# Retention's products of both heads in one run, apart from the transposes

## The chip, the cores and the metric

The kernel runs on one core of one Trainium2 chip. The metric is device time of one execution in microseconds (us), median of three runs. TensorE (PE in the profile) multiplies matrices and loads its weights in parallel with that (PEld), VectorE (DVE), ScalarE (ACT) and GpSimd (POOL) work elementwise, SyncE (SP) issues the DMAs.

## The reference, cut to what matters

A decoder trunk of two layers. Each layer projects 304 token columns (16 meta tokens, 256 prompt tokens, 8 sequences of 4 new tokens) by one input projection, runs four mixers side by side (gated delta rule, RG-LRU, GLA, retention), gates their outputs and projects them back. GLA and retention have 4 heads each, with keys of width 64 and values of width 128. Retention in its parallel form:

```python
attn = jnp.einsum('bihk,bjhk->bhij', qc, kc) * intra          # decay matrix, causal
o = (jnp.einsum('bihk,hi,bhkv->bihv', qc, from_state, s)      # what the state gives
     + jnp.einsum('bhij,bjhv->bihv', attn, vc))               # what the chunk gives
s_new = s * chunk_decay[:, None, None] + jnp.einsum('bjhk,hj,bjhv->bhkv', kc, to_state, vc)
```

GLA has the same form with a decay for each key element; each output is normalised over its 128 values (`rms_norm`).

## The kernel before

All activations lie with features on partitions and the 304 tokens on the free axis. A chunk list `CH` cuts the tokens into 128, 128 and 48.

**The main stream.** Each layer has 48 input tiles and 16 output tiles of 128 features; each takes 16 slices of weights, in 4 units of 4 slices (256 KB of weights from DRAM per unit). Weights are split into a high and a low fp32r part (`split` on ACT, tile `hi`; `low` on DVE, tile `lo`), and each slice takes three matmuls into the PSUM tile `main`. `split` runs three units ahead of its matmuls, `low` two.

**The mixers as threads.** The mixers are Python generators. While the program is written, after each slice of the main stream `bg.poll()` lets each thread that is due issue its next step, up to its next `yield`. Due times come from a model of the engines' clocks (`Clocks`, `price`), so that the order of all instructions is fixed before the chip runs. A thread is due when its last step's results are ready by the model, when ACT and DVE are not too far behind, and when one bank of its PSUM ring is free (`banks`). The rings `d` (delta threads) and `e` (all others) have three banks each; `pt(tag)` takes the next one. `price` knows the columns of a matmul, and nothing of which rows of the array it uses.

**The pair threads.** `pair_thread(l, p, m, tag)` handles two heads (p is 0 or 1 in each layer) of GLA (m = "g") or retention (m = "r"). The two heads' keys and queries share 128 partitions, head h on rows 64h to 64h+63. So the products of queries and keys (K[r], Q[r]) and what the state gives (SS[r], qe[r]) use 64 rows; transposes and all else use 128. In the trace's forms, `64*128` is such a 64-row weight, `128*128` a full one, `128*64` and `128*32` ones of 64 and 32 columns. An fp32 product is two MATMUL instructions in the trace.

Lines 1318 to 1334: for each head, per chunk a transpose of V (`ident` as other operand) and then, for retention, one product into `ps2`; then ACT copies V out and DVE multiplies the product with the decay table into `AT[h]`; POOL copies some columns of V (`copies`). Lines 1475 to 1490: for each head the output, in five products, is copied and squared by ACT (`o`, `sq`), and `o_norm` follows (a sum over partitions by `totals`, Ln, Exp, a product on DVE) before the second head's output starts. After it the thread advances its state.

GLA's pairs run one after the other in `chain()`, retention's in `rets()` after the RG-LRU; both run side by side, and beside the delta threads, whose substitution is a long run of small POOL instructions (lines 985 to 992, tiles `s9.*`).

Of the kernel before, what the change touches and what calls it, by code (L numbers as in the profile page):

```python
# [12 lines left out]
AF = mybir.ActivationFunctionType  # L13
# [5 lines left out]
T = 304  # L19
# [4 lines left out]
CH = [(0, 128), (128, 128), (256, 48)]  # L24
# [286 lines left out]
class Threads:  # L311
# [21 lines left out]
    def banks(self, tag):  # L333
        c = self.clocks
        return tag is None or all(max(c.seen(c.wrote, k), c.seen(c.read, k)) <= c.pe for k in
                                  (f"{tag}{(c.turn.get(tag, -1) + 1 + i) % 3}" for i in range(FREE)))

    def idle(self):
        self.clocks.t["P"] += 0.2
        self.poll()  # L340
# [3 lines left out]
def trunk(ctx: ExitStack, tc: tile.TileContext, I, O):  # L344
    nc = tc.nc
    clk = Clocks()
    pe, act, dve, pool, sp = (Engine(e, k, clk) for e, k in ((nc.tensor, "P"), (nc.scalar, "A"), (nc.vector, "V"),
                                                             (nc.gpsimd, "G"), (nc.sync, "S")))
# [7 lines left out]
    def tables(func):  # L356
        want = SETS.get(func)
        if want and table[0] not in want:
            nc.scalar.preload_act_table_set(want[0])  # L359
            clk.t["A"] += 1.3  # L360
            table[0] = want[0]

    def activ(out, in_, func, **kw):
        tables(func)
        act.activation(out, in_, func, **kw)
# [15 lines left out]
    def settled(*bs):  # L381
        while not all(clk.settled(b) for b in bs):
            yield
# [15 lines left out]
    eps = one.tile([128, 4], F32, name="eps")  # L399

    def C(name, a=0, n=1):
        return cst[:, CC[name] + a:CC[name] + a + n]

    def PA(name, l, a=0, n=1):
        k = PC[name, l] if (name, l) in PC else PC[name]
        return par[:, k + a:k + a + n]
# [66 lines left out]
    def choose(wide):  # L473
        w = ripe(wides)
        if wide:
            return wides, w
        m = [x for x in ripe(spare) if lent[x[1].tensor.name] >= at["e"] - HOLD]
        n = ripe(narrows)
        if m and (at["e"] < LATE or not n):
            return spare, sorted(m, key=lambda x: -lent[x[1].tensor.name])  # L480
        return (narrows, n) if n else (wides, w if len(w) > (KEEP if waits[0] < 20 else 0) else [])

    def take(n=1, wide=False):
        r = []
        while len(r) < n:
            q, c = choose(wide)
            if c:
                q.remove(c[0])
                r.append(c[0][1])
            else:  # L490
                yield
        return r if n > 1 else r[0]
# [14 lines left out]
    def give(*bs):  # L507
        for b in bs:
            q = spare if b.tensor.name in lent else wides if b.shape[1] == 384 else narrows
            q.append([clk.free(b), b])  # L510
# [24 lines left out]
    def spin(t, tag, n):  # L535
        turn[tag] = (turn.get(tag, -1) + 1) % n
        clk.slot[t.tensor.name] = f"{tag}{turn[tag]}"
        return t

    def pt(tag):  # L540
        return spin(pb.tile([128, 512], F32, tag=tag, name=tag), tag, 3)
# [42 lines left out]
    bg = Threads(clk)  # L584
# [205 lines left out]
    def stash(l, kt, o):  # L790

        if at["e"] > RETIRE and o.tensor.name not in lent and len(ripe(narrows)) >= SPARE:
            got["o", l, kt] = o
        else:
            yield from put(o_dram[:, kt, :], o[:, :T])
            give(o)
            got["o", l, kt] = None
# [45 lines left out]
    def copies(out, x, n):  # L843

        for b in range(2):
            c = TP + 16 * b
            pool.tensor_copy(out=out[:, 128 * b:128 * b + 16 * n].rearrange("p (u t) -> p u t", u=n),
                             in_=x[:, None, c:c + 16].to_broadcast([128, n, 16]))
# [11 lines left out]
    def totals(tag, sq):  # L860

        while busy:
            yield
        busy.append(1)
        hi, lo = (spin(two.tile([128, T], F32R, tag=k, name=k, bufs=1), k, 1) for k in ("hq", "lq"))
        activ(hi, sq, AF.Copy)
        yield
        dve.tensor_sub(lo, sq, hi.bitcast(F32))
        yield
        ps = pt(tag)  # L870
        pe.matmul(ps[:, :T], onesr, hi, start=True, stop=False)
        pe.matmul(ps[:, :T], onesr, lo, start=False, stop=True)
        busy.clear()
        return ps

    def o_norm(tag, l, kt, ot, sq, wcol, scale, bias, lnscale):
        ps = yield from totals(tag, sq[:, :T])
        activ(sq[:, :T], ps[:, :T], AF.Ln, scale=scale, bias=bias)
        activ(sq[:, :T], sq[:, :T], AF.Exp, scale=-0.5, bias=lnscale)
        yield  # L880
        if wcol is None:
            dve.tensor_mul(ot[:, :T], ot[:, :T], sq[:, :T])
        else:
            dve.scalar_tensor_tensor(ot[:, :T], ot[:, :T], wcol, sq[:, :T], op0=mul, op1=mul)
        yield from settled(ot)
        yield from stash(l, kt, ot)
# [362 lines left out]
    def pair_thread(l, p, m, tag):  # L1249
# [4 lines left out]
        if m == "r":  # L1254
            tab = yield from take(2)
# [15 lines left out]
        Q, K = got.pop((m + "q", l, p)), got.pop((m + "k", l, p))  # L1271
# [3 lines left out]
        qe = yield from take()  # L1275
        kt = (yield from take()) if m == "g" else None
        AT = yield from take(2)
        VT = yield from take(2, True)
# [32 lines left out]
        if m == "g":  # L1311
            ps2 = pt(tag)
            for c, (c0, n) in enumerate(CH):
                pe.matmul(ps2[:n, 2 * c:2 * c + 2], E[:, c0:c0 + n], C("hs", 0, 2), start=True, stop=True)
            activ(diag[:, 0:4], ps2[:, 0:4], AF.Copy)
            activ(diag[0:48, 4:6], ps2[0:48, 4:6], AF.Copy)
            give(E)
        for h in range(2):
            r = slice(64 * h, 64 * h + 64)
            ps = pt(tag)  # L1320
            ps2 = pt(tag) if m == "r" else None
            for c, (c0, n) in enumerate(CH):
                pe.transpose(ps[:n, 128 * c:128 * c + 128], V[h][:, c0:c0 + n], ident)
                if m == "r":
                    pe.matmul(ps2[:, c0:c0 + n], K[r, 128 * c:128 * c + 128], Q[r, c0:c0 + n], start=True, stop=True)
            activ(VT[h][:, 0:256], ps[:, 0:256], AF.Copy)
            activ(VT[h][:48, 256:384], ps[:48, 256:384], AF.Copy)
            if m == "g":
                for c, (c0, n) in enumerate(CH):
                    activ(AT[h][:, c0:c0 + n], ident[:, 0:n], AF.Copy, scale=diag[:, 2 * c + h:2 * c + h + 1])  # L1330
            else:
                dve.tensor_mul(AT[h][:, :T], ps2[:, :T], tab[h][:, :T])
            copies(V[0][:, 64 * h:], V[h], 4)
            yield
        if m == "r":
# [74 lines left out]
        ps, ps2 = pt(tag), pt(tag)  # L1410
# [17 lines left out]
        for b in range(2):  # L1428
            hm = C("hs", 0, 2)[:, :, None].to_broadcast([128, 2, 64])
            v, k = ps2[:, 128 * b:128 * b + 128], ps2[:, 256 + 128 * b:384 + 128 * b]  # L1430
# [5 lines left out]
            for h in range(2):  # L1436
                r, own = slice(64 * h + 32, 64 * h + 64), slice(64 * h, 64 * h + 64)
# [13 lines left out]
        SS = yield from take()  # L1451
        yield
        ps = pt(tag)
# [11 lines left out]
        sel = yield from take()  # L1465
# [6 lines left out]
            pool.tensor_scalar(S9[:, 0, :], S9[:, 0, :], C("dec", 3 * p + 1), None, op0=mul)  # L1472
            pool.tensor_scalar(S9[:, 1:9, :], S9[:, 1:9, :], C("dec", 3 * p + 2), None, op0=mul)
        yield
        sq = yield from take()
        for h in range(2):
            r = slice(64 * h, 64 * h + 64)
            rs = slice(64 * h, 64 * h + 48)
            ps = pt(tag)
            pe.matmul(ps[:, 0:128], VT[h][:, 0:128], AT[h][:, 0:128], start=True, stop=True)  # L1480
            pe.matmul(ps[:, 128:256], SS[r, 0:128], qe[r, 128:256], start=True, stop=False)
            pe.matmul(ps[:, 128:256], VT[h][:, 128:256], AT[h][:, 128:256], start=False, stop=True)
            pe.matmul(ps[:, 256:304], sel[:, 0:128], C("so", 48 * h, 48), start=True, stop=False)
            pe.matmul(ps[:, 256:304], VT[h][:, 256:384], AT[h][:, 256:304], start=False, stop=True)
            o = AT[h]
            activ(o[:, :T], ps[:, :T], AF.Copy)
            activ(sq[:, :T], ps[:, :T], AF.Square)
            yield
            kt_ = (8 if m == "g" else 12) + 2 * p + h
            yield from o_norm(tag, l, kt_, o, sq, PA("nc", l) if m == "g" else None, 1.0 / 128, eps[:, 0:1], 0.0)  # L1490
        give(sq, sel, SS, qe)
        advance(tag, S9, 0, 1, [(slice(64 * h, 64 * h + 64), ktb[:, 64 * h:64 * h + 64], VT[h][0:16, 256:384])
                                for h in range(2)])
        give(*VT)
# [16 lines left out]
    def skip(l):  # L1511

        return NM if l == L - 1 else 0
# [165 lines left out]
    for u, (l, ph, e, q) in enumerate(units):  # L1679
# [31 lines left out]
        c0 = skip(l) if ph == "out" or ORDER[e][0] in ("gate", "gq", "rq") else 0  # L1711
        if l == L - 1 and ph == "in" and ORDER[e][0] == "conv" and ORDER[e][1] < 4:
            c0 = NM - 4
# [19 lines left out]
        if q == NH - 1:  # L1733
# [4 lines left out]
            kind, i = ORDER[e]  # L1738
# [12 lines left out]
    k = 0  # L1751
    for n in (1, 1, 2, 4, 4, 4):
        g = xf[:, k:k + n, :]
# [94 lines left out]
```

## Time and profile before

| | |
|---|---|
| median of three runs | 1128.61 us (1127.08 to 1130.58) |
| profiled execution, its own time | 1128.37 us |
| its span, first to last instruction | 1126.4 us |
| TensorE busy | 1075.5 us, 95% of the span |
| VectorE, ScalarE, GpSimd busy | 66%, 57%, 41% |
| mean granted TensorE clock | 0.983 of full |

Busy time of an engine is the union of its instructions. A MATMUL's recorded length is longer than the time for which it keeps the next one back; the distance from one start to the next is what counts. All helpers record their instructions at line 298, so that rows are told apart by tile names: `e<-cst,n` is a matmul into ring e with the identity (in `cst`) and a buffer named n.

### The profile page before, as it was taken

The numbers are of one execution on the slowest core, as the hardware profiler recorded it, in microseconds if no ns is written. First come the engines' busy times: TensorE is split into PE (matmuls) and PEld (weight loads), VectorE is DVE, ScalarE is ACT, GpSimd is POOL, SyncE is SP. The second block draws the span as 40 slices with busy tenths as digits, with TensorE's granted clock in tenths as the row PEclk, the third lists the DMA queues.
The fourth block names the chain that finished last, engine by engine and source line by source line (L and its number), as shares of the span: only waits on it lengthen the run. The fifth ranks groups of instructions, "written<-read, shape, count | busy, mean of one in ns | idle before, by whom it ended". The sixth has DMA issues, their size and how long they took to land.

```text
span 1126.4 us, 22838 instructions
## 1 busy us (share of the span) xinstructions
PE 1075.5 (95%) x7974; PEld 1008.6 (90%) x7974; DVE 746.9 (66%) x1449; ACT 638.2 (57%) x1432; POOL 462.4 (41%) x947
## 2 busy tenths in 40 slices
PE   8999989998999999899999998999899999999996
PEld 7998979887999899899999998889789989899995
DVE  6866578678567555566568755787975575666564
ACT  6677934554754475444455875546466457645442
POOL 5423387424426833212122348554444583321110
PEclk8999989999999999899999999999999999999998
DMA  6554535455457454566544554335464755565663
GB/s 212 182 161 160 156 97 160 149 188 152 140 182 222 130 185 141 168 208 196 185 148 150 173 159 159 114 114 169 152 187 131 240 155 187 152 203 178 192 191 141
DMA packets 117058, 187.78 MB, mean 167 GB/s; under 512 B 22176, under 2 KB 45456, under 8 KB 116944
## 3 DMA queue, kind: packets, MB, share of 16 engines
q1 hardware_dynamic: 116944, 186.34, 53.5%
q8 instruction: 62, 1.02, 0.4%
q14 instruction: 52, 0.43, 0.1%
HBM read 165.09 MB, written 19.95 MB: 164 GB/s over the span
## 4 chain that ended last, share of the span: by engine, by line
PE 66%; POOL 11%; DVE 9%; DMA 5%; issue 4%; ACT 3%; SPq 1%; DVEq 0%; POOLq 0%; ACTq 0%
PE main L298 52%; PE e L298 7%; PE d L298 7%; DVE lo L298 3%; POOL s9.4_168 L298 3%; DMA raw<-in_w_in_dram 2%; POOL s9.3_11274 L298 2%; POOL n L298 2%; DVE n L298 2%; POOL m L298 1%; POOL s9.0_6106 L298 1%; DVE m L298 1%; DVE zq L298 1%; SPq L298 1%; DVE acc L298 1%
## 5 line engine op out<-in xcount | busy, mean ns | idle before, releaser
L298 PE MATMUL main<-xh,hi 128*128 128x304 f32 (+2 forms) x1488 | 471.8, 317 | 2.2 <-ACT xh L298 2.2
L298 PE MATMUL main<-xh,lo 128*128 128x304 f32 (+2 forms) x1488 | 453.0, 304 | 11.5 <-DVE lo L298 11.3
L298 DVE TENSOR_TENSOR lo<-raw,hi 128x512 fp32r<-128x512 f32 (+1 forms) x513 | 389.0, 776 | 111.8 <-ACT hi L298 104.0
L298 ACT ACTIVATE hi<-raw 128x512 fp32r<-128x512 f32 (+1 forms) x513 | 317.5, 626 | 251.5 <-PE main L298 113.1
L298 PE MATMUL main<-xl,hi 128*128 128x304 f32 (+2 forms) x1488 | 450.5, 303 | 0.3 <-DVE xl L298 0.2
L298 PEld LDWEIGHTS main<-xh,hi 128*128 128x128 f32 x1488 | 284.0, 191 | 16.4 <-issue 8.7
L298 PEld LDWEIGHTS main<-xh,lo 128*128 128x128 f32 x1488 | 283.9, 191 | 16.5 <-DVE lo L298 16.4
L298 PEld LDWEIGHTS main<-xl,hi 128*128 128x128 f32 x1488 | 284.6, 191 | 2.8 <-DVE xl L298 1.1
L298 PE MATMUL main<-m,hi 128*128 128x304 f32 (+1 forms) x1024 | 211.3, 301 | 0.0
L298 PEld LDWEIGHTS main<-m,hi 128*128 128x128 f32 x1024 | 168.1, 190 | 3.7 <-issue 2.9
L298 PE MATMUL main<-m,lo 128*128 128x304 f32 (+1 forms) x512 | 154.4, 302 | 2.0 <-DVE lo L298 2.0
L298 POOL TENSOR_TENSOR ssq<-ssq,n 128x304 f32<-128x304 f32 (+1 forms) x29 | 34.9, 1203 | 175.6 <-ACT n L298 175.6
L298 PEld LDWEIGHTS main<-m,lo 128*128 128x128 f32 x512 | 96.9, 189 | 2.2 <-DVE lo L298 2.2
L298 POOL COPY cvo<-ct 128x3 f32<-128x3 f32 x64 | 32.4, 534 | 116.1 <-DVE ct L298 116.0
L298 POOL TENSOR_TENSOR n<-n,n 128x304 f32<-128x304 f32 (+1 forms) x38 | 35.1, 937 | 91.6 <-ACT n L298 65.4
L298 ACT ACTIVATE n<-n 128x304 f32<-128x304 f32 (+4 forms) x114 | 47.8, 439 | 42.6 <-DVE n L298 34.4
L298 DVE TENSOR_TENSOR n<-main,n 128x304 f32<-128x304 f32 (+1 forms) x32 | 14.9, 466 | 62.7 <-PE main L298 47.6
L298 DVE SCALAR_TENSOR_TENSOR acc<-ct,par,acc 128x328 f32<-128x328 f32 x64 | 42.7, 667 | 6.1 <-ACT acc L298 4.8
L298 ACT ACTIVATE m<-m 128x304 f32<-128x304 f32 (+6 forms) x101 | 42.1, 433 | 5.4 <-PE d L298 3.2
L359 ACT ACT_TABLE_LOAD x33 | 42.3, 1283 | 0.6
L298 ACT ACTIVATE n<-e 128x304 f32<-128x304 f32 (+5 forms) x65 | 19.3, 307 | 28.0 <-PE e L298 13.8
L298 DVE TENSOR_TENSOR n<-main,rstd 128x304 f32<-128x304 f32 (+1 forms) x40 | 18.6, 464 | 24.8 <-PE main L298 24.7
(410 smaller groups left out, 1410.5 us busy)
## 6 DMA issues: line engine op xcount, KB each, us to landing
raw<-in_w_in_dram SPq DMA_DIRECT2D x383, 256.0 KB
raw<-in_w_out_dram SPq DMA_DIRECT2D x128, 256.0 KB
n<-o_dram SPq DMA_DIRECT2D x27, 152.0 KB
m<-in_x_dram SPq DMA_DIRECT2D x16, 152.0 KB
o_dram<-m SPq DMA_DIRECT2D x16, 152.0 KB
n<-in_x_dram SPq DMA_DIRECT2D x16, 152.0 KB
xs_dram<-n SPq DMA_DIRECT2D x16, 152.0 KB
n<-xs_dram SPq DMA_DIRECT2D x16, 152.0 KB
```

What stands on the lines that cost most here:

```text
L298: r = f(*a, **k)
L359: nc.scalar.preload_act_table_set(want[0])
```

## The change

For retention, the products of queries and keys of both heads are issued first, chunk by chunk with the heads in turn, into two banks, one for each head; the products with the decay tables follow; after a yield each head's transposes run by themselves. For GLA and retention, the outputs of both heads are issued in one run: first what the state gives, for both heads, then all else, head by head; both squares have a buffer of their own, and the two `o_norm` follow. Ahead of both runs `vacant(tag, 2)` makes the thread yield until two banks of its ring are free by the model.

```diff
+    def vacant(self, tag, n):
+        c = self.clocks
+        while not all(max(c.seen(c.wrote, k), c.seen(c.read, k)) <= c.pe for k in
+                      (f"{tag}{(c.turn.get(tag, -1) + 1 + i) % 3}" for i in range(n))):
+            yield
...
-        for h in range(2):
-            r = slice(64 * h, 64 * h + 64)
+        if m == "r":
+            yield from bg.vacant(tag, 2)
+            ps2 = [pt(tag), pt(tag)]
+            for c, (c0, n) in enumerate(CH):
+                for h in range(2):
+                    r = slice(64 * h, 64 * h + 64)
+                    pe.matmul(ps2[h][:, c0:c0 + n], K[r, 128 * c:128 * c + 128], Q[r, c0:c0 + n],
+                              start=True, stop=True)
+            for h in range(2):
+                dve.tensor_mul(AT[h][:, :T], ps2[h][:, :T], tab[h][:, :T])
+            yield
+        for h in range(2):
             ps = pt(tag)
-            ps2 = pt(tag) if m == "r" else None
             for c, (c0, n) in enumerate(CH):
                 pe.transpose(ps[:n, 128 * c:128 * c + 128], V[h][:, c0:c0 + n], ident)
-                if m == "r":
-                    pe.matmul(ps2[:, c0:c0 + n], K[r, 128 * c:128 * c + 128], Q[r, c0:c0 + n], start=True, stop=True)
             activ(VT[h][:, 0:256], ps[:, 0:256], AF.Copy)
             activ(VT[h][:48, 256:384], ps[:48, 256:384], AF.Copy)
...
-            else:
-                dve.tensor_mul(AT[h][:, :T], ps2[:, :T], tab[h][:, :T])
             copies(V[0][:, 64 * h:], V[h], 4)
             yield
...
-        sq = yield from take()
+        sqs_ = yield from take(2)
+        yield from bg.vacant(tag, 2)
+        ps = [pt(tag), pt(tag)]
         for h in range(2):
             r = slice(64 * h, 64 * h + 64)
-            rs = slice(64 * h, 64 * h + 48)
-            ps = pt(tag)
-            pe.matmul(ps[:, 0:128], VT[h][:, 0:128], AT[h][:, 0:128], start=True, stop=True)
-            pe.matmul(ps[:, 128:256], SS[r, 0:128], qe[r, 128:256], start=True, stop=False)
-            pe.matmul(ps[:, 128:256], VT[h][:, 128:256], AT[h][:, 128:256], start=False, stop=True)
-            pe.matmul(ps[:, 256:304], sel[:, 0:128], C("so", 48 * h, 48), start=True, stop=False)
-            pe.matmul(ps[:, 256:304], VT[h][:, 256:384], AT[h][:, 256:304], start=False, stop=True)
-            o = AT[h]
-            activ(o[:, :T], ps[:, :T], AF.Copy)
-            activ(sq[:, :T], ps[:, :T], AF.Square)
-            yield
+            pe.matmul(ps[h][:, 128:256], SS[r, 0:128], qe[r, 128:256], start=True, stop=False)
+        for h in range(2):
+            pe.matmul(ps[h][:, 128:256], VT[h][:, 128:256], AT[h][:, 128:256], start=False, stop=True)
+            pe.matmul(ps[h][:, 0:128], VT[h][:, 0:128], AT[h][:, 0:128], start=True, stop=True)
+            pe.matmul(ps[h][:, 256:304], sel[:, 0:128], C("so", 48 * h, 48), start=True, stop=False)
+            pe.matmul(ps[h][:, 256:304], VT[h][:, 256:384], AT[h][:, 256:304], start=False, stop=True)
+            activ(AT[h][:, :T], ps[h][:, :T], AF.Copy)
+            activ(sqs_[h][:, :T], ps[h][:, :T], AF.Square)
+        yield
+        for h in range(2):
             kt_ = (8 if m == "g" else 12) + 2 * p + h
-            yield from o_norm(tag, l, kt_, o, sq, PA("nc", l) if m == "g" else None, 1.0 / 128, eps[:, 0:1], 0.0)
-        give(sq, sel, SS, qe)
+            yield from o_norm(tag, l, kt_, AT[h], sqs_[h], PA("nc", l) if m == "g" else None, 1.0 / 128, eps[:, 0:1],
+                              0.0)
+            give(sqs_[h])
+        give(sel, SS, qe)
```

## Rows read from the trace of the kernel before

**Rows 1.** The page: busy us of each engine; the chain that ended last, by engine.
```profile
PE 1075.5 (95%) x7974; PEld 1008.6 (90%) x7974; DVE 746.9 (66%) x1449; ACT 638.2 (57%) x1432; POOL 462.4 (41%) x947
PE 66%; POOL 11%; DVE 9%; DMA 5%; issue 4%; ACT 3%; SPq 1%; DVEq 0%; POOLq 0%; ACTq 0%
```

**Rows 2.** The waits of PE: total us, times, longest us.
```profile
PE main L298 <- DVE lo L298: 13.3, 17, 2.7
...
PE d L298 <- POOL s9.0_6076 L298: 4.0, 1, 4.0
```

**Rows 3.** Timeline of PE, one retention head: start us, us, instruction, xcount.
```profile
280.32 0.30 PE L298 MATMUL main<-xl,hi 128*128 128x304 f32 x1
280.45 0.30 PE L298 MATMUL main<-xh,lo 128*128 128x304 f32 x1
280.59 0.27 PE L298 MATMUL e<-cst,n 128*128 128x128 f32 x1
280.80 0.48 PE L298 MATMUL e<-m,g 64*128 64x128 f32 x2
281.21 0.33 PE L298 MATMUL e<-cst,n 128*128 128x128 f32 x1
...
282.45 0.41 PE L298 MATMUL main<-xh,hi 128*128 128x304 f32 x1
282.70 0.30 PE L298 MATMUL main<-xl,hi 128*128 128x304 f32 x1
```

**Rows 4.** Timeline of PE, the outputs of two heads of one GLA pair.
```profile
301.48 0.30 PE L298 MATMUL main<-xh,lo 128*128 128x304 f32 x1
301.62 0.39 PE L298 MATMUL e<-n,g 128*128 128x128 f32 x2
301.93 0.48 PE L298 MATMUL e<-n,n 64*128 64x128 f32 x2
...
304.76 0.30 PE L298 MATMUL main<-xl,hi 128*128 128x304 f32 x1
```

**Rows 5.** Groups of PE by form: count, busy us, mean ns.
```profile
L298 PE MATMUL e<-n,n 64*128 64x128 f32 x20 | 4.9, 323 | 0.0
...
L298 PE MATMUL e<-n,g 64*128 64x48 f32 x8 | 1.7, 290 | 0.0
```

**Rows 6.** Timeline of PE, products that use 64 and 32 columns of the array.
```profile
275.85 0.66 PE L298 MATMUL e<-g,n 128*64 128x128 f32 x8
276.44 0.41 PE L298 MATMUL main<-xh,hi 128*128 128x304 f32 x1
...
283.07 0.86 PE L298 MATMUL e<-s9.4_168,lxg 128*32 128x128 f32 x18
```

**Rows 7.** Timeline of PE, transposes alone.
```profile
288.28 0.51 PE L298 MATMUL e<-cst,g 128*128 128x128 f32 x3
288.63 0.60 PE L298 MATMUL e<-cst,n 128*128 128x128 f32 x4
```

**Rows 8.** The chain by line in the stretches 275:325, 340:395 and 875:920.
```profile
by line: PE main L298 60.7%; PE e L298 30.8%; PE d L298 7.4%; DVE lo L298 1.4%; issue 0.1%
...
by line: POOL s9.4_168 L298 44.1%; POOL n L298 12.7%; issue 10.7%; POOL s9.3_4455 L298 7.7%; DMA n<-m 5.9%; DMA g<-dx 4.6%; SPq L298 4.3%; POOL g L298 2.6%; POOL lxr L298 2.1%; POOL m L298 1.5%; DVE lo L298 1.3%; ACT hi L298 1.2%; DVE lq L2
...
by line: POOL s9.3_11274 L298 53.6%; POOL n L298 11.9%; issue 11.6%; DMA s9.3_11274<-in_xid_dram 9.5%; SPq L298 3.7%; POOL g L298 2.6%; PE main L298 2.6%; POOL m L298 1.7%; DVE lo L298 1.5%; PE e L298 1.3%; POOLq L298 0.7%; DVE n L298 0.1%
```

**Rows 9.** Timeline of PE, a transpose behind POOL in 901:922.
```profile
919.03 0.56 PE L298 MATMUL e<-cst,n 128*128 128x128 f32 x3 [0.15 <-POOL n L298]
```

**Rows 10.** Timelines of ACT and DVE: evacuation of an output, of a product.
```profile
303.25 0.42 ACT L298 ACTIVATE n<-e 128x304 f32<-128x304 f32 x1 [1.77 <-PE e L298]
...
282.56 0.47 DVE L298 TENSOR_TENSOR n<-e,m 128x304 f32<-128x304 f32 x1 [2.30 <-PE e L298]
```

**Rows 11.** Busy us (x) of PE, PEld, DVE, ACT, POOL in a stretch; granted clock, DMA.
```profile
460.00:465.00 5.00, 3.56 (x13) 3.37 (x13) 4.21 (x5) 0.32 (x1) 1.39 (x1) 0.50 0.34 118
465.00:470.00 5.00, 5.00 (x32) 5.00 (x32) 1.17 (x2) 1.26 (x2) 0.00 (x0) 0.85 0.83 269
```

## The prediction

> **What bounds the kernel now.** I read the page first: TensorE is busy for 95% of the span, and 66% of the chain that ended last is TensorE, far ahead of POOL with 11% and VectorE with 9% [rows 1]. The list of PE's waits comes next: what it waits for is small and scattered, 13.3 us in 17 waits for `lo`, one of 4.0 us for POOL [rows 2]. So time on TensorE's own queue is the first suspect, but "busy" there is a union of lengths that overlap, and does not say how long one instruction keeps the next back. For that I went to the timeline of single instructions, start to start, at the places that the diff touches, and last to the chain in the stretches where these places lie, because TensorE's time is worth something only where the chain runs over it.
>
> The timeline shows what the average hides. The main stream goes 0.14 us from start to start (280.32 to 280.45). One retention head takes from the main matmul at 280.45 to the second one behind it at 282.70, 2.25 us; without the two main steps of 0.14 that is 1.97 us [rows 3]. Its work is far less. A transpose by itself takes 0.35/3 = 0.12 us, three of them from 288.28 to 288.63 [rows 7]. A product of 128 columns is two instructions of about the same size; as an estimate I take 0.11 each, and 0.15 us for the two of 48 columns. So three transposes (0.33), two products (0.43) and the short one (0.15) are 0.91 us. The other 1.06 us lie between neighbours of different forms: transpose, product, transpose, product, transpose, product, main are six changes between a full array and 64 rows, 0.18 us each. One such change is seen directly: from the product at 280.80 to the transpose at 281.21 it is 0.41 us for two instructions of 0.11.
>
> The Trainium skill has this as a rule ("TensorEngine Tiling (Array Packing)", Key Properties: changing the tiling mode drains TensorE, changing only the tile doesn't). The trace agrees, with the 0.18 us; the sum below uses only the row.
>
> **The change part by part.**
>
> *Products of retention.* Two heads now cost 2 x 1.97 = 3.94 us. Afterwards there are two pieces. The transposes are six, without a change of form: 6 x 0.11 = 0.66 us. The products are one block with one change in and one out, 0.36 to 0.4 us, and twelve instructions. Here is the first open price: whether two products on different rows of the array run at the same time. No row here shows that. What rows show is the other direction: eight instructions of 64 columns take 0.59 us to the next main start, and eighteen of 32 columns 0.86 us in all [rows 6]; one behind the other at 0.11 they would be 0.88 and 1.98 us. So instructions on different columns share the time. The bounds are full sharing, half of 2 x 0.58 = 0.58 us for the products, and none, 1.2 us with some of the short ones' weight loads in the open. I take sharing, because that is the nearest row: the heads alternate, and they write to two banks. The block is then 0.97 us, or 1.6 us without sharing, and a pair saves 3.94 - 0.66 - 0.97 = 2.3 us, or 1.65 us.
>
> The same skill page (Gotcha 1) says that different row tiles may not write the same PSUM bank at the same time; the change does use two banks. It also holds that row tiles run side by side, and by that the block is the 0.97 us.
>
> There are four pairs (two layers, two pairs each): the rows of the short form, this and another of eight, are 16 instructions, two for each of eight heads [rows 5].
>
> *Outputs.* Two heads take from 301.48 to 304.76, less two main steps, 3.00 us [rows 4]; all heads have this form, eight pairs with GLA's (of the four rows of the 64*128 form with 128 columns, 20 + 16 + 16 + 12 = 64 instructions, 32 are these [rows 5]). The work of a head is ten instructions, about 1.03 us; the two heads' four changes take the rest, 0.94 us, 0.23 each. Afterwards there are two changes (0.47), the state's products together (0.21, or 0.43 without sharing), and twice 0.82 us of the rest: 2.32, or 2.54 us. A pair saves 0.68, or 0.46 us.
>
> *What is added.* No instruction and no DMA; SP's and POOL's queues hold the same work in the same order, `copies` a step later than before. `vacant` waits only while the order is written; on the chip it is no wait. There is one more step and one more buffer for each pair. Behind the retention block DVE has two evacuations of 0.47 us in a row instead of one, and behind the outputs ACT has four of 0.42 us in a row instead of two [rows 10]. What queues behind these are `lo` and `hi`, which run two and three units (of at least 12 x 0.14 = 1.7 us each) ahead, so up to 0.5 and 0.9 us of delay lie inside 3.4 and 5 us of cover. I cost them at nothing; without the cover, 0.9 us at each of eight places would be 7 us.
>
> *Where it counts.* All of it would be 4 x 2.3 + 8 x 0.68 = 14.6 us. In 275:325, where a first retention pair and a GLA pair lie, the chain is 99% TensorE; there each saved microsecond counts [rows 8]. The second pair of each layer lies elsewhere: in 340:395 and in 875:920 the chain runs over POOL, through the substitution of the delta thread (`s9.4_168` 44%, `s9.3_11274` 54%), with TensorE at 3% or less [rows 8]. In 875:920 PE comes out of that stretch with a wait of 0.15 us for POOL at 919.03 [rows 9]; it would wait 2.3 us more if its products were done earlier. So I leave the two second pairs' products out (2 x 2.3), and half of one output (0.35): 14.6 - 4.95 = 9.7 us. Without sharing the same sum is 2 x 1.65 + 8 x 0.46 - 0.25 = 6.7 us.
>
> The sum is made against the profiled execution, 1128.4 us, which is within 0.3 us of the median of the runs. **1128.4 - 9.7 = 1118.7 us.**
>
> **The rivals.** *No sharing.* The changes of form go, but the two heads' products run one behind the other: 1128.4 - 6.7 = 1121.7 us. For it: no row shows two row halves at once. Against it: the column rows [rows 6]. Chance 0.14.
>
> *All of it counts.* The second pairs fall to places where TensorE decides, because the extra step moves them past the substitution: 1128.4 - 14.6 = 1113.8 us. Against it: in both layers the second pair lay in that stretch. Chance 0.12.
>
> *The gain is hidden, or one new stall eats it.* The model prices the changed work differently in time (two waits for banks, another step), so every later step can fall elsewhere. One matmul put ahead of its operand is dear: the wait of 4.0 us for `s9.0_6076` [rows 2] is followed by a slow stretch: PE had been idle, and the granted clock is 0.50 in 460:465, which is 1.2 of 2.4 GHz, and 0.85 in 465:470 [rows 11]. That loses 2.5 us and 5 x 0.15 = 0.75 us, less half of the 1.4 us in which PE was idle anyway (busy 3.56 of 5), so 2.6 us more. One such stall more leaves 1118.7 + 6.6 = 1125.3 us, at the edge of what can be told from no change. The same result comes if the delta thread's end decides the layer and TensorE only waits longer for it: then nothing is won, 1128.4 us. The skill's page warns of a third way (PSUM Bottleneck: tiling speeds up TensorE but not the evacuation of PSUM); here that would mean that ACT's run of four makes `hi` late, and by the 7 us above gives 1118.7 + 7 = 1125.7 us. For this case: all waits of [rows 2] are of this kind. Against it: the old order has as many chances to lose such a stall as to win one. Chance 0.19 in all.
>
> *Slower.* The same mechanism twice: the new order puts two more matmuls on operands of POOL that are late by 4 us, the likeliest place being a retention state's scaling on POOL beside the substitution. At 6.6 us each it is 1118.7 + 13.2 = 1131.9 us, 3.5 over the profiled execution; it decides from the second such stall on. Against it: only one of PE's waits is this long for a single POOL tile of the delta thread [rows 2]. Chance 0.10.
>
> **How the numbers follow.** The forecast has 0.45. A measurement of this kernel can tell about 0.3%, 3.4 us, from no change. Faster by more than that are the forecast, no sharing and all of it, and a little of the hidden case: 0.72. Within it: 0.18. Slower: 0.10. The range for 8 in 10 goes down to 1110, the case in which all counts and half a stall goes away, and up to 1129, where the hidden case ends and the slower one, and a little of the hidden one, are left out. The forecast's own range is 1115 to 1122.
>
> **What would show it.** In the timeline after: a block of twelve 64*128 instructions with no transpose in it, of about 1 us (sharing: pairs of starts some ns apart) or 1.6 us (none); transposes alone at 0.11; the outputs of a pair in 2.3 us between main matmuls. The changes of form fall from 16 to 4 for a retention pair (six for each head's products, two for each output, before) and from 4 to 2 for a GLA pair. In 340:395 and 875:920 the waits of PE for POOL grow. Wrong would be: main steps behind the block longer than 0.25 us, waits for `hi` or `lo` that grow by more than a few us in total, or a new wait of over 4 us with the clock at 0.50 behind it.

## The result, and the profile after

The changed kernel takes 1112.5 us (median of four runs, 1108.92 to 1113.57) against 1129.59 us for the kernel before on the same chip: the ratio is 0.9844, with an interval of 0.9821 to 0.9868. That is 17 us less; forecast were 9.7 us, with 1118.7 us as the time and 1110 to 1129 as the range. The profiled execution took 1113.57 us, 14.8 less than that of before, and the rows below are to be held against this 14.8.

The page after, busy time of each engine and the chain by engine, answers to [rows 1].

```profile
PE 1062.6 (96%) x7974; PEld 1001.4 (90%) x7974; DVE 740.6 (67%) x1449; ACT 641.6 (58%) x1436; POOL 458.4 (41%) x947
PE 69%; POOL 8%; DVE 8%; DMA 6%; ACT 4%; issue 3%; SPq 1%; DVEq 0%; ACTq 0%; POOLq 0%
```

TensorE is busy for 12.9 us less with as many instructions, and it is still what bounds the kernel. Its waits (total us, times, longest us) answer to [rows 2].

```profile
PE main L298 <- DVE lo L298: 10.3, 13, 2.7
PE e L298 <- POOL n L298: 7.7, 4, 4.2
...
```

The wait of 4.0 us for `s9.0_6076` is not in the list any more. The waits for POOL's `n` are longer (before: 4.7 us in 3). Those for `lo` fell by 3 us, and in 272:300, where a block of products and two runs of outputs stand, the list of TensorE's waits is empty: DVE's two evacuations in a row made nothing late there.

The timeline of PE at a first retention pair (start us, us, instruction, xcount) answers to [rows 3] and [rows 7].

```profile
275.42 0.30 PE L298 MATMUL main<-xh,lo 128*128 128x304 f32 x1
275.65 0.87 PE L298 MATMUL e<-m,g 64*128 64x128 f32 x12
276.45 0.41 PE L298 MATMUL main<-xh,hi 128*128 128x304 f32 x1
276.70 0.30 PE L298 MATMUL main<-xl,hi 128*128 128x304 f32 x1
...
277.66 0.30 PE L298 MATMUL main<-xh,lo 128*128 128x304 f32 x1
277.80 0.49 PE L298 MATMUL e<-cst,n 128*128 128x128 f32 x3
278.05 0.39 PE L298 MATMUL main<-xh,hi 128*128 128x304 f32 x1
278.27 0.30 PE L298 MATMUL main<-xl,hi 128*128 128x304 f32 x1
```

All twelve instructions of the products stand in one block without a transpose. From the main matmul ahead of it to the second one behind it are 1.28 us; less two main steps of 0.14 that is 1.00 us. A head's transposes stand alone, from 277.80; from 277.66 to 278.27, less two main steps, they take 0.33 us, 0.11 each. Inside the group of twelve the trace's single records start in pairs, at 275.864 and 275.871, 275.976 and 275.982, 276.087 and 276.094: 6 to 7 ns apart, and each pair 0.11 us behind the last. So the two heads' products, on different rows of the array, share the time.

The timeline of PE at the outputs of a pair answers to [rows 4].

```profile
299.27 0.30 PE L298 MATMUL main<-xh,lo 128*128 128x304 f32 x1
299.50 0.49 PE L298 MATMUL e<-n,n 64*128 64x128 f32 x4
299.92 0.71 PE L298 MATMUL e<-n,g 128*128 128x128 f32 x4
...
301.72 0.39 PE L298 MATMUL main<-xh,hi 128*128 128x304 f32 x1
301.95 0.30 PE L298 MATMUL main<-xl,hi 128*128 128x304 f32 x1
```

What the state gives stands once, as x4, instead of twice as x2, with one change of form in and one out. From 299.27 to 301.95, less two main steps, are 2.40 us instead of 3.00. The state's products share the time as well: their single records start at 299.495 and 299.502, then at 299.708 and 299.715.

**Where the time went.** The kernel has four phases, cut at the first matmul of each: the input tiles of layer 0, its output tiles, the same of layer 1. In the table by stretches the columns are the stretch, its length, then busy us (x instructions) of PE, PEld, DVE, ACT and POOL, the granted clock and the DMA's share and rate. First the kernel before, then the changed one.

```profile
0.00:455.60 455.60, 437.79 (x3225) 405.50 (x3226) 308.00 (x630) 277.93 (x645) 217.72 (x473) 0.98 0.54 163
455.60:576.70 121.10, 117.11 (x801) 111.09 (x799) 69.82 (x102) 55.16 (x100) 23.99 (x18) 0.97 0.60 192
576.70:1010.20 433.50, 417.27 (x3178) 389.87 (x3178) 302.32 (x615) 257.50 (x604) 204.47 (x440) 0.99 0.52 161
1010.20:1126.40 116.20, 103.32 (x774) 102.17 (x772) 66.80 (x103) 47.56 (x84) 16.23 (x16) 0.97 0.56 179
```

```profile
0.00:455.20 455.20, 432.61 (x3227) 403.16 (x3228) 310.87 (x633) 279.87 (x646) 218.06 (x474) 0.98 0.53 163
455.20:570.00 114.80, 114.43 (x800) 108.58 (x798) 66.34 (x99) 55.32 (x101) 21.66 (x17) 1.00 0.64 204
570.00:996.30 426.30, 410.92 (x3179) 385.95 (x3179) 296.56 (x615) 258.98 (x606) 202.56 (x440) 0.99 0.53 163
996.30:1111.70 115.40, 104.63 (x774) 103.72 (x772) 66.78 (x103) 47.48 (x84) 16.13 (x16) 0.97 0.55 178
```

Three readings. In layer 0's input phase TensorE is busy 5.2 us less (437.79 to 432.61) and idle 4.8 us more (17.8 to 22.6), so that the phase is only 0.4 us shorter. In layer 0's output phase, which the change does not touch, 6.3 us are gone: 3.6 us of idle time and 2.7 us of busy time, with the granted clock at 1.00 instead of 0.97. In layer 1's input phase 7.2 us are gone, of which 6.4 are busy time.

The first reading has its place at layer 0's second retention pair (timeline of PE; in brackets the idle time before a group and what ended it).

```profile
360.50 0.49 PE L298 MATMUL e<-cst,g 128*128 128x128 f32 x3
362.09 0.33 PE L298 MATMUL e<-cst,n 128*128 128x128 f32 x1 [1.10 <-POOL n L298]
364.55 0.90 PE L298 MATMUL e<-cst,n 128*128 128x128 f32 x3 [2.13 <-POOL n L298]
```

The granted clock of the 5 us from 365 is 0.50; in the kernel before it is 1.00 throughout 340:395. From 338 to 364.6 the chain is 53% the substitution `s9.4_168` and 15% `n`, both on POOL. This is the stretch that [rows 8] showed for before. PE's waits for POOL's `n` in 340:395 say what becomes of saved time there. The four lines are, from the top, the kernel before, the changed kernel, and two experiments told below: tfirst_p1, where this pair takes 1.3 us less than in the kernel before, and kq_back_p1, where it takes 2.0 us more than in the changed kernel.

```profile
PE e L298 <- POOL n L298: 0.4, 1, 0.4
PE e L298 <- POOL n L298: 3.2, 2, 2.1
PE e L298 <- POOL n L298: 1.6, 1, 1.6
PE e L298 <- POOL n L298: 1.3, 1, 1.3
```

In tfirst_p1 what is saved comes back as a wait (1.2 of 1.3 us), and in kq_back_p1 what is added comes off it (1.9 of 2.0 us); each line is of a single profile.

The second reading is an order on POOL's queue. In the kernel before, POOL's timeline ahead of the output phase is this:

```profile
450.51 2.35 POOL L298 TENSOR_TENSOR s9.4_6059<-n,cst 128x1024 fp32r<-128x1024 f32 x1
457.69 1.61 POOL L298 TENSOR_TENSOR n<-n,n 128x304 f32<-128x304 f32 x2 [4.84 <-ACT n L298]
459.26 2.13 POOL L298 TENSOR_TENSOR s9.0_6076<-n,cst 128x1024 fp32r<-128x1024 f32 x1
```

And in the changed kernel:

```profile
441.75 2.13 POOL L298 TENSOR_TENSOR s9.4_6014<-n,cst 128x1024 fp32r<-128x1024 f32 x1
443.85 2.12 POOL L298 TENSOR_TENSOR s9.0_6047<-n,cst 128x1024 fp32r<-128x1024 f32 x1
457.76 1.64 POOL L298 TENSOR_TENSOR n<-n,n 128x304 f32<-128x304 f32 x2 [11.80 <-ACT n L298]
```

Before, the second of two such tiles stood behind two additions that waited for ACT until 457.69, and came at 461.4; TensorE waited 4.0 us for it, and the slow stretch of [rows 11] followed. Now it stands ahead of the additions and is done at 446.0; TensorE reads it at 453.10 without a wait. No line of the diff moves it: the planner wrote another order.

### The profile page after: what moved, and what is told of

Same layout as the page of the kernel before. It is cut to its first block, busy times and chain, and to the rows that moved or that the text cites. A ratio compares the mean times of both kernels' runs of the same rounds, so it can differ in the third digit from the quotient of the medians.

```text
span 1111.7 us, 22856 instructions
## 1 busy us (share of the span) xinstructions
PE 1062.6 (96%) x7974; PEld 1001.4 (90%) x7974; DVE 740.6 (67%) x1449; ACT 641.6 (58%) x1436; POOL 458.4 (41%) x947
## 4 chain that ended last, share of the span: by engine, by line
PE 69%; POOL 8%; DVE 8%; DMA 6%; ACT 4%; issue 3%; SPq 1%; DVEq 0%; ACTq 0%; POOLq 0%
PE main L298 55%; PE e L298 7%; PE d L298 7%; DMA raw<-in_w_in_dram 4%; POOL s9.4_168 L298 4%; DVE lo L298 3%; DVE m L298 1%; POOL s9.2_3660 L298 1%; POOL m L298 1%; ACT hi L298 1%; SPq L298 1%; DVE n L298 1%; ACT n L298 1%; DVE acc L298 1%; ACT m L298 1%
## 5 line engine op out<-in xcount | busy, mean ns | idle before, releaser
L298 ACT ACTIVATE n<-n 128x304 f32<-128x304 f32 (+4 forms) x121 | 50.6, 439 | 35.6 <-DVE n L298 26.5
L298 DVE SCALAR_TENSOR_TENSOR acc<-ct,par,acc 128x328 f32<-128x328 f32 x64 | 45.1, 705 | 8.8 <-ACT acc L298 7.4
L298 ACT ACTIVATE m<-m 128x304 f32<-128x304 f32 (+5 forms) x94 | 38.9, 431 | 7.1 <-PE d L298 3.7
```

The source lines that it names most:

```text
L298: r = f(*a, **k)
```

## The experiments

Each time stands against the kernel before on the same chip: 4 to 12 executions of each kernel against 11 or 35 of the kernel before, intervals of 95%. "In the old order" means that the planner (`Clocks`) is told of the calls as they were, and the changed ones are issued without its knowledge, so that all other instructions keep their order on every engine. This is done by two switches:

```diff
-            r = f(*a, **k)
+            r = f(*a, **k) if self.emits else None
...
-            self.clocks.op(self.kind, price(self.kind, name, size(out), out, cols), [out], ins)
+            self.counts and self.clocks.op(self.kind, price(self.kind, name, size(out), out, cols), [out], ins)
```

**Changes of form alone, in the old order: tfirst, tfirst_p0, tfirst_p1.** The kernel before, with a head's three transposes ahead of its three products: two changes of form instead of six. In all pairs, in the first pair of each layer, in the second pair of each layer (`True`, `p == 0`, `p == 1`).

```diff
+            flip = m == "r" and True
+            pe.emits = not flip
             for c, (c0, n) in enumerate(CH):
...
+            if flip:
+                pe.emits, pe.counts = True, False
+                for c, (c0, n) in enumerate(CH):
+                    pe.transpose(ps[:n, 128 * c:128 * c + 128], V[h][:, c0:c0 + n], ident)
+                for c, (c0, n) in enumerate(CH):
+                    pe.matmul(ps2[:, c0:c0 + n], K[r, 128 * c:128 * c + 128], Q[r, c0:c0 + n], start=True, stop=True)
+                pe.counts = True
```

> The kernel before with one thing changed: in each retention head the three transposes come first and the three products behind them. Every other instruction and its order on every engine stay as before (the model of the engines is told the old order). Each of eight heads has two changes of form instead of six; at 0.18 us each that is 8 x 4 x 0.18 = 5.8 us of TensorE. Theory A, all of TensorE's time counts wherever it is saved: 5.8 us faster than before. Theory B, as predicted, the second pairs' share is lost to waits for POOL: 2.9 us faster. Theory C, the gain of the whole change was the new order of all instructions and not the changes of form: no difference.

> As the run with transposes first, but only in the first retention pair of each layer. Theories A and B: 2.9 us faster. Theory C: no difference.

> As the run with transposes first, but only in the second retention pair of each layer. Theory A: 2.9 us faster. Theory B: no difference, and the waits of PE for POOL or for the DVE instructions behind it grow by as much as is saved, in 340:395 and 875:920. Theory C: no difference.

Measured: tfirst 1127.72 us, ratio 0.9977 (0.9961 to 0.9993); tfirst_p0 1127.71, 0.9980 (0.9966 to 0.9995); tfirst_p1 1131.70, 1.0014 (0.9994 to 1.0034). A head in tfirst, timeline of PE:

```profile
276.22 0.30 PE L298 MATMUL main<-xh,lo 128*128 128x304 f32 x1
276.36 0.49 PE L298 MATMUL e<-cst,n 128*128 128x128 f32 x3
276.77 0.86 PE L298 MATMUL e<-m,g 64*128 64x128 f32 x6
277.57 0.41 PE L298 MATMUL main<-xh,hi 128*128 128x304 f32 x1
```

From main to main are 1.35 us where it was 2.00, so four changes cost 0.65 us. The first pairs alone give 2.3 us of the 2.6 that their four heads save on TensorE; the second pairs give nothing, and in their trace the waits for POOL's `n` are 6.8 us in 4 instead of 4.7 in 3, so that 2.1 of the 2.6 us that they save come back as waits. The granted clock has a part in it too: its median is 0.9825 over tfirst_p1's runs and 0.985 over those of before, which is some 2.8 us (an estimate, 0.0025 of the span, as if TensorE were the bound throughout). All pairs together give 2.6 us, not 5.2. The changes of form are what costs, and on this evidence the first pairs' lie on the path and the second pairs' don't.

**Each half with a new order: kq_only, out_only.** The first hunk of the diff without the second, and the reverse; the planner writes the order anew.

> The first half of the change alone: retention's products of both heads in a run of their own; the outputs as before. The order of all instructions is planned anew. From the trace after, a block costs 1.00 us and a head's transposes 0.34, so a pair goes from 3.94 to 1.67 us: 4 x 2.27 = 9.1 us if all counts (theory A), 4.5 us if the second pairs don't (theory B), in both cases plus or minus what the new order does to the waits. Theory C: anything, without the shorter blocks deciding it.

> The second half of the change alone: the outputs of both heads of a pair in one run; retention's products as before. The order of all instructions is planned anew. A pair's outputs take 2.40 us instead of 3.00, so 8 x 0.60 = 4.8 us by the changes of form alone (theory A and B, but for half of one output in a stretch that POOL decides). The first half alone gave 2.8 us. If the two halves simply add up to the 17 us of the whole, this one gives 14 us, of which 4.8 are explained and the rest would be the new order (theory C); if it gives 5 us, the whole has a gain that neither half has.

Measured: kq_only 1127.62 us, ratio 0.9977 (0.9961 to 0.9993), 2.6 us; out_only 1118.98, 0.9910 (0.9885 to 0.9934), 10.2 us. Neither is its share of TensorE's time (4.5 and 4.8 us). In kq_only the late POOL tile is still there, as in the kernel before:

```profile
PE d L298 <- POOL s9.0_6078 L298: 3.3, 1, 3.3
```

Its output phase takes 121.9 us, against 121.1 before. That it gains less than its share goes with the clock: the granted clock of its twelve runs is 0.977 to 0.982 with a median of 0.980, that of before has a median of 0.985, some 5.6 us (an estimate, as above). No run tells why this order gets the lower clock. In out_only the wait is gone and the output phase takes 114.8 us, as in the changed kernel. So the order that the planner writes with the second hunk is what brings the 6.3 us.

**The changed kernel in its own order, with one part undone: in_rows, out_old, and after_again beside them.** in_rows issues all products of the first head, then all of the second; out_old issues the output products in their old order, head by head with two changes of form each; after_again is the changed kernel.

```diff
+            pe.emits = False
...
+            pe.emits, pe.counts = True, False
+            for h in range(2):
+                for c, (c0, n) in enumerate(CH):
+                    r = slice(64 * h, 64 * h + 64)
+                    pe.matmul(ps2[h][:, c0:c0 + n], K[r, 128 * c:128 * c + 128], Q[r, c0:c0 + n],
+                              start=True, stop=True)
+            pe.counts = True
```

```diff
+        pe.emits = False
...
+        pe.emits, pe.counts = True, False
+        for h in range(2):
+            r = slice(64 * h, 64 * h + 64)
+            pe.matmul(ps[h][:, 0:128], VT[h][:, 0:128], AT[h][:, 0:128], start=True, stop=True)
+            pe.matmul(ps[h][:, 128:256], SS[r, 0:128], qe[r, 128:256], start=True, stop=False)
+            pe.matmul(ps[h][:, 128:256], VT[h][:, 128:256], AT[h][:, 128:256], start=False, stop=True)
...
+        pe.counts = True
```

> The changed kernel with one thing taken back: in the run of products the three chunks of one head come first and the other head's behind, not in turn. Everything else and its order stay as in the changed kernel. If instructions on different rows share the time only while they are neighbours, a block goes from 1.03 us between main matmuls to about 1.5 us, 0.5 us each, 1 us in the two first pairs and at most 2 us in all against the changed kernel. If they share however they are ordered, no difference.

> The changed kernel with one thing taken back: in the run of both heads' outputs the matmuls stand in their old order, each head's state product between its other products. Everything else and its order stay as in the changed kernel. Four changes of form for a pair instead of two, 3.0 instead of 2.4 us, 8 x 0.6 = 4.8 us slower than the changed kernel if TensorE decides at all these places, 4.5 if not at one half of one pair. If the gain of the whole is the new order (theory C), it stays at most of the 17 us below the kernel before.

> The changed kernel itself, to set the others of this call against it on the same chip. 16 to 17 us below the kernel before, as measured.

Measured: after_again 1111.17 us, ratio 0.9842 (0.9817 to 0.9867); in_rows 1113.71, 0.9855 (0.9832 to 0.9877); out_old 1116.64, 0.9883 (0.9864 to 0.9903). Between the ratios, the old order of the outputs costs 0.0041 or 4.6 us (give or take 3.6, from the two intervals), and in its trace a pair takes 3.06 us from main to main where the changed kernel has 2.46: 8 x 0.60 = 4.8 us. Not taking turns costs 1.5 us, which can't be told from nothing. Its block, timeline of PE:

```profile
274.92 0.30 PE L298 MATMUL main<-xh,lo 128*128 128x304 f32 x1
275.15 1.20 PE L298 MATMUL e<-m,g 64*128 64x128 f32 x12
276.27 0.41 PE L298 MATMUL main<-xh,hi 128*128 128x304 f32 x1
```

It takes 1.35 us from main to main where the block in turns takes 1.03, so taking turns is worth 0.32 us for a pair, and little of the gain.

**The changes of form put back: kq_back, kq_back_p1.** The changed kernel in its own order, with four full matmuls (eight instructions) added to each pair's block, which write two columns that nothing reads: eight changes of form instead of two. In all pairs, and in the second pairs alone (`p == 1` for `True`).

```diff
+                    if h == 0 and c < 2 and True or h == 1 and c > 0 and True:
+                        pe.counts = False
+                        pe.matmul(ps2[h][:, 304:306], ident, ident[:, 0:2], start=True, stop=True)
+                        pe.counts = True
```

> The changed kernel with the cost of its runs of products put back and nothing else: between the products of each run stand four matmuls of a full array onto two unused columns, so that a run has eight changes of form and costs about as much more as the change saved there, 2.2 us (an estimate: six changes of 0.18, four small matmuls of 0.15 to 0.2, and the shared time lost). Their results are not read. Every other instruction keeps its order. If all of it counts (theory A): 4 x 2.2 = 9 us slower than the changed kernel. If the second pairs' share is lost to waits (theory B): 4.5 us. If the gain of the products was the new order alone (theory C): 0. What then remains below the kernel before, beyond the 4.6 us of the outputs, is the new order's.

> As the run with the products' cost put back, but only in the second pair of each layer. Theory A: 4.5 us slower than the changed kernel. Theory B: no difference beyond 1 us. Results that no one reads are the only addition.

Measured: kq_back 1120.56 us, ratio 0.9901 (0.9883 to 0.9918); kq_back_p1 1109.60, 0.9827 (0.9810 to 0.9845). The start of a block in kq_back, timeline of PE:

```profile
274.68 0.30 PE L298 MATMUL main<-xh,lo 128*128 128x304 f32 x1
274.91 0.48 PE L298 MATMUL e<-m,g 64*128 64x128 f32 x2
275.32 0.38 PE L298 MATMUL e<-cst 128*128 128x2 f32 x2
275.63 0.49 PE L298 MATMUL e<-m,g 64*128 64x128 f32 x4
...
277.70 0.39 PE L298 MATMUL main<-xh,hi 128*128 128x304 f32 x1
```

The block takes 3.02 us where it was 1.03, 1.99 more. In the second pairs, where it costs TensorE 4.0 us in all, it costs no time (the ratio is 0.0015 lower than the changed kernel's, 1.7 us, give or take 3.5); the 1.9 us that came off the wait in 340:395 are part of the reason, and a granted clock of 0.988 instead of 0.985 (medians) is worth some 3.3 us (an estimate, as above). In all pairs it costs 0.0059 more, 6.7 us; the 4.0 us that the first pairs' blocks take longer lie within the two intervals (3.5 us), and so would a price of some 8 us for all pairs; but that is excluded by kq_back_p1, where half of it costs nothing. The granted clock of kq_back's runs has a median of 0.9825 against 0.985 in after_again's. Its profile puts part of the loss into one stretch, windows of 5 us:

```profile
827.00:832.00 5.00, 4.12 (x34) 3.49 (x33) 4.15 (x13) 3.01 (x10) 2.12 (x10) 1.00 0.43 165
832.00:837.00 5.00, 5.00 (x33) 4.02 (x31) 3.79 (x8) 2.03 (x8) 3.04 (x6) 0.76 0.59 157
837.00:842.00 5.00, 5.00 (x36) 4.47 (x36) 0.88 (x2) 1.45 (x4) 3.44 (x4) 0.56 0.21 57
```

TensorE waits 0.88 us for `lo` at 831.6, and in the block behind it, layer 1's first, the granted clock falls; that loses 5 x 0.24 + 5 x 0.44 = 3.4 us. All of what kq_back costs in its profile lies in layer 1's input phase (434.0 us, 7.7 more than in the changed kernel); layer 0's is 454.8 us, no longer than without the added work.

**The order alone: before_m, after_m.** One constant of the planner is 0.22 instead of 0.20, in the kernel before and in the changed one; the work is the same.

```diff
-MARGIN = 0.2
+MARGIN = 0.22
```

> The kernel before with another order of the same instructions and nothing else: the model's margin between a step's end and its next due time is 0.22 us instead of 0.20. If the order alone moves the time by several us (theory C, and what is left over in A and B), this run differs from before by 3 to 8 us either way, with waits of other sizes at other places; if orders are alike, by less than 2 us.

> The changed kernel with the margin of 0.22 us: another order of its instructions. If the changed kernel's order is a lucky one, this is 3 to 8 us slower than the changed kernel; if orders are alike, by less than 2 us, and it stays 16 us or more below before.

Measured: before_m 1136.83 us, ratio 1.0049 (1.0034 to 1.0064); after_m 1136.02, 1.0055 (1.0036 to 1.0074). Another order costs the kernel before 5.5 us and the changed kernel some 24 us (0.0213 against after_again's ratio). With this constant the change is worth nothing that can be measured. The waits of PE in after_m:

```profile
PE main L298 <- DVE lo L298: 14.9, 22, 3.0
PE main L298 <- ACT hi L298: 5.1, 4, 2.6
PE d L298 <- ACT hq L298: 4.4, 2, 2.2
...
PE d L298 <- POOL s9.3_6080 L298: 2.9, 1, 2.9
```

Waits that the changed kernel has shorter or not at all: 4.6 us for `lo`, 4.5 for `hi`, 4.4 for `hq`, and a late POOL tile again. Where they pile up the clock falls too (windows of 5 us of after_m):

```profile
455.00:460.00 5.00, 2.06 (x8) 1.47 (x7) 1.61 (x3) 1.19 (x3) 2.67 (x2) 0.50 0.00 0
460.00:465.00 5.00, 4.44 (x15) 3.95 (x15) 2.02 (x4) 3.31 (x6) 1.05 (x2) 0.54 0.06 24
```

The granted clock of its six runs is 0.969 to 0.979. Its block of products and its runs of outputs are as short as the changed kernel's (1.03 and 2.46 us from main to main); what it saves there it loses in the order. Its output phase of layer 0 takes 120.7 us: the code of the second hunk is there, and the 6.3 us are not.

## Why the prediction was right, and where it was not

The time lay in the range and the sign was right; the forecast gain of 9.7 us was 7 us short.

*What binds.* Right: TensorE's queue, and in it the distance from start to start. A change between 64 rows and the full array costs about what was read from [rows 3], 0.18 us: tfirst takes four changes out of a head and saves 0.65 us, 0.16 each; kq_back adds six changes and eight instructions of some 0.11 us to a block, parts one product of each head from its neighbour (2 x 0.11 us that were shared) and makes the block 1.99 us longer, (1.99 - 0.88 - 0.22) / 6 = 0.15. By the Trainium skill ("TensorEngine Tiling (Array Packing)", Key Properties) only the mode drains TensorE, not the tile. This case agrees: the changed kernel's block goes to and fro between the two row halves, and pair follows pair at 0.11 us, the step of instructions that change nothing.

*Products of retention.* Right in mechanism and size: the block was to take 0.97 us with sharing and takes 1.00; a pair was to save 2.3 us and saves 3.94 - 0.66 - 1.00 = 2.28. The rival without sharing is out, by the pairs of starts some ns apart. Its price of 1.6 us for the block stands in no run: in_rows has 1.32, but two of its instructions still overlap (last section); with 2 x 0.11 us for these it would be about 1.54, an estimate.

*Outputs.* The term was mis-sized: 0.60 us saved for a pair, not 0.68, so 4.8 us for eight instead of 5.4. What was too high is the 0.23 us for a change: with the shared 0.22 us taken off, two changes are 0.38 us, 0.19 each. out_old measured 4.6 us, give or take 3.6.

*What is added.* Right: nothing became late by the evacuations in a row. ACT's four after the outputs stand where `hi` has its cover; TensorE's waits for `hi` are 0.6 us in all.

*Where it counts.* Right for the second pairs: tfirst_p1 and kq_back_p1 change their time on TensorE by 2.6 and by 4.0 us, neither moves the end by as much as can be told from nothing, and in 340:395 the waits for POOL's `n` take up nearly all of it. For layer 1's second pair it is less clear: in 860:930 these waits go from 0.2 to 1.1 us in tfirst_p1, and in kq_back_p1 all waits for POOL there fall from 1.0 us to 0.3; how the rest of the 1.3 and 2.0 us went is not shown. The waits in 340:395 grew from 0.4 to 3.2 us in the changed kernel, as the prediction said. One reading was off: by [rows 8] TensorE has 3.9% of the chain in 875:920 (2.6 + 1.3), not 3% or less; nothing in the sum hangs on it. Too generous for the rest of layer 0: in the profiles its input phase kept the 0.4 us of some 7 us that were taken from its TensorE work (two pairs' products and four outputs, 2 x 2.3 + 4 x 0.6), since TensorE got longer waits for POOL and, in this execution, half clock in return. kq_back, too, paid nothing in this phase. These are single profiles, and two of the changed kernel differ by 1.4 us there; tfirst_p0's 1.6 us, out of 1.3 due in this phase, speak the other way. How much of layer 0's input phase counts is left open.

*The rivals, and the step that failed.* The forecast had the mechanism's sum and an order that neither wins nor loses. The order was treated as a source of stalls alone; that the old order's own stall could go was named in half a sentence ("as many chances to lose such a stall as to win one"), and went into the range as half a stall. That is the step that failed: the order's part was put at nothing in the sum. The stall went entirely, and with about the price worked out there, 6.6 us: the output phase of layer 0 is 6.3 us shorter. In the fourteen traces this phase takes 114.8 us in seven (the changed kernel twice, the four experiments in its order, and out_only) and 120.4 to 121.9 us in the other seven (the kernel before, tfirst and its two parts, kq_only, before_m and after_m). With the sizes as measured the prediction's sum is 2 x 2.28 + 7.5 x 0.60 = 9.1 us, and with the 6.3 us 15.4 of the measured 17. That sum is as good as its parts: by the profiles layer 0's input phase gave less than its part (0.4 us), and layer 1's more (7.2, where one pair and four outputs make 4.7). The difference of 2.5 us was not traced to single instructions.

So the gain has two causes. The changes of form are shown, by undoing them: 4.6 us for the outputs, and for the first pairs' products between 2.3 us (tfirst_p0, which takes out four of a head's six changes) and 6.7 us (kq_back, with a lower clock in it). The vanished stall is shown by its place in the traces and by which kernels have it; after_m, with the second hunk and 120.7 us, shows that it belongs to the planner's order and not to the change, and before_m and after_m show how far an order alone can move the time. That the order came out this way is luck, and so is how far the measured gain went past the forecast: with the margin of 0.22 the same change gains nothing, and its 1136 us lie above the range.

## What to carry to other kernels

Count the changes between array forms from start to start, not from busy time; products that use half of the rows go together, and the transposes go elsewhere. Saved TensorE time counts only where the chain runs over TensorE: add the cost to one place at a time, in an order that is held fixed, to see which places count. Where a planner writes the order, a change of the code is two changes; hold the order fixed to price the one, and try some neighbouring orders before the other is credited to the code.

## What was not expected of the hardware

Twelve products on two row halves overlap even where the program issues one half's six ahead of the other's. In in_rows the single records of starts are 275.474 and 275.480, then 275.585, 275.693 and 275.697, and the first record of 48 columns comes after six of 128 columns, although the first head has only four ahead of its short ones: so two instructions of the second head started while the first head still had some to go. With them the block is 0.32 us longer than with the heads in turn; one behind the other throughout it would be some 0.54 us longer, an estimate.
